# Modulation chunks in pairs of 1024 columns on VectorE, and layer 0's second-gate chunks moved to VectorE

## The chip, the cores and the metric

One core of one Trainium2 chip runs the whole program in one launch. The metric is the time of one execution on the device in microseconds (us); less is better. Time before: 3164.56 us, the median of 3 runs (3164.38 to 3165.99).

## The reference

Two layers of a diffusion backbone on a latent and a context stream of 256 tokens each, 2048 channels, everything in float32. Layer 0 mixes tokens by pooling in four groups of 512 channels (windows 2, 4, 8, 16); layer 1 is neighbourhood attention. Both are followed by a gated feed-forward block with 5504 inner channels. What the change touches is the modulation: in front of and behind every sub-layer stand a shift, a scale and a gate per channel, which come from one vector for each stream:

```
sc  = silu(c)            # latent stream, 2048 values;  silu(c_ctx) for the context stream
mod = sc @ w_mod[l] + b_mod[l]          # (2048) x (2048, 6 * 2048) for each layer l
shift1, scale1, gate1, shift2, scale2, gate2 = split(mod, 6)
h = h + gate1 * mixer(rms_norm(h, g1) * (1 + scale1) + shift1)
h = h + gate2 * conv_ffn(rms_norm(h, g2) * (1 + scale2) + shift2)
```

The matrix w_mod holds 2 x 2048 x 12288 float32 values, 201 MB, each of which is used once for each stream.

## The kernel before

**Layout.** Channels lie on the 128 partitions, so the 2048 channels are 16 tiles (KT). Matrix products run as three float32r products: every piece of weights (512 KB, 128 x 1024) is loaded by SP's queue into a room (`stage`), ScalarE makes its high part (L142, names ending in h) and VectorE the low part (L144, names ending in l); TensorE then does high x high, high x low, low x high. The rooms are 6 tiles of a staging pool (`wst`) and, in the first part of layer 0, tiles of the inputs A0 to A15 that aren't in use yet; `lend` says which. A room comes free when its last reader is done, and SP's queue is in order, so a transfer that waits for a room holds all later ones.

**Chunks.** The 12288 columns of a layer's modulation are 24 chunks of 512: chunks 0 to 3 are the first shift, 4 to 7 the first scale, 8 to 11 the first gate, 12 to 15, 16 to 19 and 20 to 23 the same for the second norm. A chunk's weights are 16 blocks of 128 x 512, 4 MB in 8 transfers. There are two ways to work one off:
- `mod_pe` (layer 0, all 24 chunks): 16 float32 matmuls with the 32-column tile `sc` as weights (L193), four side by side on quarters of the array, into one PSUM bank; then a copy by ScalarE (L198), four transposes on TensorE (L203), a reduction (L205) and the bias (L181) on VectorE.
- `mod_pieces` (layer 1): VectorE multiplies each 128 x 512 block by the stream's value per partition and adds it to `macc` (L219 for the first block, L221 for the rest). Chunks 0 to 7 are done for both streams (`two`, 32 instructions each), chunks 8 to 23 for the latent stream alone (`one`, 16 each). At a chunk's end VectorE transposes `macc` in blocks of 32 (L228) and reduces it (L229, tile `modr`); one small matmul with `quad` sums the quarters of the partitions (L165, tile `modt_<chunk>s`, issued ahead of other work by `tc.high_priority`), and VectorE adds the bias (L181).

**Order.** Both are generators, and each `next` on them issues one step (a quarter of a chunk). Layer 0's mixer and the first 8 feed-forward tiles run in four groups g = 0 to 3 (`partial`, 32 half tiles each): within group g TensorE contracts the 512 channels of that group (tiles `cg` and `cu`, weights `wcg`, `wcu`), while the mixer of group g + 1 and its chunks (`need`) are issued between the half tiles (`between`). The inputs `Ad` of group g + 1 come out of that mixer. In group 3 the chunks still open are the four of the second gate (20 to 23). The end of group 3 on VectorE is `late` (L328). After that come the other feed-forward tiles: for each four of them `gu0` (gate and up products, L601 to L603, PSUM banks `gu`), then `down0` in four parts mg (L625 to L627, weights `wd_0` to `wd_3`, banks `d`), and every such step takes one step of `mod_pieces` with it. The bank tag `d` has three banks and a fourth from tag `m`, taken in turn by the down tiles and the sums `modt`. Then the tile scheduler of the language orders the instructions of each engine; each engine runs its own in that order.

Of the kernel before, what the change touches and what calls it, by code (L numbers as in the profile page):

```python
# [10 lines left out]
F32 = mybir.dt.float32  # L11
F32R = mybir.dt.float32r
# [24 lines left out]
# half tiles of the last group at which the second norm and the first gates are done  # L37
# [3 lines left out]
# columns of the packed per-channel array: (name, columns)  # L41
# [16 lines left out]
def kernel(ctx: ExitStack, tc: tile.TileContext, xT, cxT, wmod, wg, wu, wd, wp,  # L58
# [35 lines left out]
    # silu(c), silu(c_ctx)  # L94
# [25 lines left out]
    def load(src, cols, name):  # L120
        """[128, cols] in pieces of up to 1024 columns"""
# [8 lines left out]
    def split(ts, name, share=0):  # L130
        """float32 pieces -> list of (hi, lo); share: one lo in so many on GpSimd"""
# [24 lines left out]
    def by_row(ps):  # L156
        """four transposed tiles whose columns 32 j + s hold four parts of stream s: [128, 4, s, j]"""
        return ps.rearrange("p (i j c) -> p i c j", i=4, j=4)[:, :, 0:2, :]

    def quarter_sum(x, n, name):  # L160
        """x: [32 j + c, (tile, b), n streams], parts j of the sum for the channel 32 b + c of the tile; for each
        quarter of the partitions a view [32 channels, tiles, streams]"""
        with tc.high_priority():
            ps = bank("d", f"{name}s")
            nc.tensor.matmul(ps[:, : 16 * n].rearrange("p (k s) -> p k s", s=n), quad, x, start=True, stop=True)  # L165
# [3 lines left out]
    def finish_mod(l, ch, streams, src):  # L169
        """bias added to the views of quarter_sum; scales turn into factors"""  # L170
# [16 lines left out]
    def mod_pe(l, ch, sc, pool):  # L187
        """512 columns of one modulation matrix, both streams, on TensorE"""
# [19 lines left out]
    def mod_pieces(todo, pool):  # L208
        """the same for the chunks of todo, on VectorE, one weight piece per step"""
        for l, ch, streams in todo:  # L210
            acc = {s: pool.tile([P, 512], F32, tag=f"macc{s}", bufs=1, name=f"macc{s}_{l}_{ch}") for s in streams}
            for g in range(4):
                ts = load(lambda a, b: wmod[l, ch, g, :, a:b], 2048, f"wm{l}_{ch}_{g}")
                for j in range(4):
                    k = 4 * g + j
                    w = ts[j // 2][0][:, 512 * (j % 2) : 512 * (j % 2) + 512]
                    for s in streams:
                        if k == 0:
                            nc.vector.tensor_scalar(acc[s], w, sc2[:, k, s : s + 1], None, op0=ALU.mult)  # L219
                        else:  # L220
                            nc.vector.scalar_tensor_tensor(acc[s], w, sc2[:, k, s : s + 1], acc[s],  # L221
                                                           op0=ALU.mult, op1=ALU.add)
                if g == 3:
                    n = len(streams)
                    r = pool.tile([P, 16, 2], F32, tag="modr", bufs=2, name=f"modr_{l}_{ch}")[:, :, 0:n]
                    for s in streams:
                        t = f0.tile([P, 512], F32, tag="t2", name=f"modu{s}_{l}_{ch}")
                        nc.vector.transpose(t, acc[s])  # L228
                        nc.vector.tensor_reduce(out=r[:, :, s], in_=t.rearrange("p (k r) -> p k r", r=32), axis=AX.X,  # L229
                                                op=ALU.add)  # L230
                yield
            finish_mod(l, ch, streams, quarter_sum(r, n, f"modt_{l}_{ch}"))
# [5 lines left out]
    class Norm:  # L238
        """sum of squares over channels, fed one channel tile at a time; then 1 / rms on all partitions"""
# [37 lines left out]
    def normalise(l, which, h_of, streams, rstd, pool, ks=range(KT), keep=A):  # L277
        """A[k] = float32r parts of rstd * h * (1 + scale) * g + shift, per stream"""
# [15 lines left out]
    # ================= layer 0 =================  # L294
# [879 lines left out]
```

## Time and profile before

| what | us |
|---|---|
| median of 3 runs | 3164.56 |
| span of the profiled execution | 3160.8 |
| what lies around the span, against the median | 3.8 |
| first loads and group 0's chunks and mixer | 0 to 80 |
| group 0 of layer 0 (first to last product on its inputs, about) | 80 to 167 |
| groups 1, 2, 3 (about) | 167 to 257, 257 to 348, 348 to 440 |
| other feed-forward tiles of layer 0 without modulation steps | 440 to 617 |
| the same with steps of `mod_pieces` | 617 to 1700 |
| layer 1: attention, feed-forward | 1740 to 2390, 2390 to 3160 |

The profile is of one execution, whose own time isn't given apart from its span. TensorE (PE) is busy for 97% of the span and its granted clock is 0.990 of full speed, so the span is read as TensorE's work plus the places where TensorE waits. VectorE (DVE) is busy for 64%. A row of a group says: line, engine, operation, output <- inputs, shape, count, then busy time and mean duration of one in ns, then the engine's idle time ahead of it and what ended it.

### The profile page before, as it was taken

How to read it: one execution, taken by the hardware profiler on the slowest of the kernel's cores; microseconds unless marked ns; L12 is line 12 of the kernel's file. 1: busy time of each engine (PE TensorE's matmuls, PEld its weight loads, DVE VectorE, ACT ScalarE, POOL GpSimd, SP SyncE). 2: the span in 40 equal slices, each digit the busy share in tenths (PEclk: the TensorE clock that was granted, in tenths of full speed). 3: DMA queues.
4: the chain of work that ended last, by engine and by line, in shares of the span. 5: the costliest groups of instructions: out<-in, count | busy, mean ns of one | idle time of the engine just before them, and what ended most of it. 6: DMA issues, size and time to landing. Idle time of an engine off the chain costs nothing.

```text
span 3160.8 us, 40908 instructions
## 1 busy us (share of the span) xinstructions
PE 3064.6 (97%) x15082; PEld 2410.6 (76%) x15082; DVE 2037.9 (64%) x2886; ACT 1353.6 (43%) x2187; POOL 940.3 (30%) x843
## 2 busy tenths in 40 slices
PE   6999999999999999999999999999999999999998
PEld 2565568887877778777787777777778888888887
DVE  4445664387686775868675665574777676666666
ACT  3333454323333232323324443343445665556665
POOL 2011213303123040413313000000002477667776
PEclk9999999999999999999999999999999999999999
DMA  9878663375564655556563333232345555555553
GB/s 376 330 270 315 207 206 100 111 229 183 170 199 159 202 171 189 187 167 199 164 202 114 102 105 106 96 109 94 104 141 179 176 193 184 196 185 182 180 182 119
DMA packets 161545, 559.72 MB, mean 177 GB/s; under 512 B 17600, under 2 KB 22208, under 8 KB 161344
## 3 DMA queue, kind: packets, MB, share of 16 engines
q1 hardware_dynamic: 161344, 557.10, 52.9%
q8 instruction: 119, 1.95, 0.2%
q14 instruction: 82, 0.67, 0.1%
HBM read 554.93 MB, written 2.10 MB: 176 GB/s over the span
## 4 chain that ended last, share of the span: by engine, by line
PE 69%; DVE 12%; DMA 12%; issue 4%; POOL 2%; ACT 1%; SPq 0%; DVEq 0%; POOLq 0%; ACTq 0%
DMA wm<-wmod 11%; DVE macc L221 6%; PE g L731 5%; PE u L731 4%; PE d L776 4%; PE mod L193 3%; PE d L627 3%; PE d L625 3%; PE d L626 3%; PE g L732 3%; PE u L732 2%; PE d L777 2%; PE k L895 2%; PE k L896 2%; PE q L915 2%
## 5 line engine op out<-in xcount | busy, mean ns | idle before, releaser
L221 DVE SCALAR_TENSOR_TENSOR macc<-wm,sc,macc 128x512 f32<-128x512 f32 x480 | 411.9, 883 | 225.7 <-DMA wm<-wmod 221.2
L638 POOL TENSOR_TENSOR hl<-hl,dy 128x256 f32<-128x256 f32 x160 | 164.8, 1030 | 931.5 <-ACT dy L637 930.6
L788 POOL TENSOR_TENSOR hl<-hl,dy 128x256 f32<-128x256 f32 x320 | 323.2, 1044 | 45.3 <-ACT dy L786 43.7
L637 ACT ACTIVATE dy<-d,modT 128x256 f32<-128x256 f32 x320 | 133.2, 470 | 172.7 <-PE d L627 162.1
L638 POOL TENSOR_TENSOR hc<-hc,dy 128x256 f32<-128x256 f32 x160 | 180.1, 1125 | 0.0
L193 PE MATMUL mod<-wm,sc 128*32 128x512 f32 x768 | 135.9, 613 | 24.6 <-DMA wm<-wmod 24.6
L344 ACT ACTIVATE sg<-g 128x512 f32<-128x512 f32 x43 | 27.2, 632 | 299.0 <-DVE g L341 299.0
L869 POOL TENSOR_TENSOR rk<-rk,rp 128x256 f32<-128x256 f32 x16 | 12.7, 795 | 372.8 <-DVE rk L868 314.4
L786 ACT ACTIVATE dy<-d,modT 128x512 f32<-128x512 f32 x160 | 103.5, 686 | 29.8 <-PE d L777 24.8
L439 POOL TENSOR_TENSOR pf<-ws,inv 128x256 f32<-128x256 f32 x32 | 28.4, 906 | 221.4 <-DVE ws L434 153.0
L144 DVE TENSOR_TENSOR wd_2l<-wd,wd_2h 128x1024 fp32r<-128x1024 f32 (+1 forms) x44 | 57.0, 1300 | 46.5 <-ACT wd_2h L142 45.7
L193 PEld LDWEIGHTS mod<-wm,sc 128*32 128x32 f32 x768 | 23.7, 109 | 80.8 <-issue 58.1
L755 DVE TENSOR_TENSOR actb<-sgb,actb 128x256 fp32r<-128x256 f32 x43 | 68.2, 1586 | 20.8 <-ACT actb L754 20.2
L627 PE MATMUL d<-act,wd_0l 128*128 128x512 f32 x172 | 69.7, 406 | 12.1 <-DVE wd_0l L144 12.1
L144 DVE TENSOR_TENSOR wd_0l<-wd,wd_0h 128x1024 fp32r<-128x1024 f32 (+1 forms) x44 | 53.9, 1227 | 37.8 <-ACT wd_0h L142 37.1
L142 ACT CAST wd_0h<-wd 128x1024 fp32r<-128x1024 f32 (+1 forms) x44 | 45.3, 1031 | 67.9 <-PE g L602 35.9
L626 PE MATMUL d<-act,wd_0h 128*128 128x512 f32 x172 | 69.1, 402 | 0.0
L625 PE MATMUL d<-act,wd_3h 128*128 128x512 f32 x172 | 68.0, 395 | 1.1 <-DVE modT L181 1.1
L625 PE MATMUL d<-act,wd_0h 128*128 128x512 f32 x172 | 69.0, 402 | 0.0
L625 PE MATMUL d<-act,wd_2h 128*128 128x512 f32 x172 | 67.9, 395 | 0.1
L626 PE MATMUL d<-act,wd_2h 128*128 128x512 f32 x172 | 68.0, 395 | 0.0
L627 PE MATMUL d<-act,wd_1l 128*128 128x512 f32 x172 | 68.0, 395 | 0.0
(1753 smaller groups left out, 10024.1 us busy)
## 6 DMA issues: line engine op xcount, KB each, us to landing
wm<-wmod SPq DMA_DIRECT2D x384, 512.0 KB, 5.2
wd<-wd SPq DMA_DIRECT2D x168, 512.0 KB, 4.5
wg<-wg SPq DMA_DIRECT2D x156, 512.0 KB, 4.0
wu<-wu SPq DMA_DIRECT2D x156, 512.0 KB, 4.7
wv<-wv SPq DMA_DIRECT2D x32, 512.0 KB, 3.6
wk<-wq SPq DMA_DIRECT2D x32, 512.0 KB, 3.8
wq<-wq SPq DMA_DIRECT2D x32, 512.0 KB, 3.7
wo<-wo SPq DMA_DIRECT2D x32, 512.0 KB, 3.7
```

The costliest lines, as they stand in the source:

```text
L144: eng.tensor_tensor(lo[:, :n], t[:, :n], hi[:, :n].bitcast(F32), op=ALU.subtract)
L193: nc.tensor.matmul(ps[32 * j : 32 * j + 32, :], sc[:, 4 * g + j, :], ts[j // 2][0][:, 512 * (j % 2) : 512 * (j % 2) + 512], start=(g == 0) ...
L221: nc.vector.scalar_tensor_tensor(acc[s], w, sc2[:, k, s : s + 1], acc[s], op0=ALU.mult, op1=ALU.add)
L625: nc.tensor.matmul(ps, hi[:, o : o + P], xh, start=(i == 0), stop=False)
L626: nc.tensor.matmul(ps, hi[:, o : o + P], xl, start=False, stop=False)
L627: nc.tensor.matmul(ps, lo[:, o : o + P], xh, start=False, stop=(i == n - 1))
L637: nc.scalar.activation(y[:, s], ps[:, T * s : T * s + T], AF.Copy, scale=M(0, 5, k, s))
L638: nc.gpsimd.tensor_tensor(h_of(s)[:, k, :], h_of(s)[:, k, :], y[:, s], op=ALU.add)
L731: nc.tensor.matmul(ps, hi[:, c : c + P], flat(B[k]), start=(k == 0), stop=False)
L732: nc.tensor.matmul(ps[:, T:], lo[:, c : c + P], B[k][:, 0], start=False, stop=(k == KT - 1))
L776: nc.tensor.matmul(ps, hi[:, o : o + P], flat(acts[i]), start=(i == 0), stop=False)
L788: nc.gpsimd.tensor_tensor(hl[:, k, :], hl[:, k, :], y[:, q], op=ALU.add)
```

## The change

Three things change.
1. `mod_pieces` becomes `mod_pairs`. The latent-only chunks 8 to 23 of layer 1 are done two at a time: a transfer brings one block of two neighbouring chunks (two rows of 2 KB for each partition instead of one of 4 KB), and one instruction works on 128 x 1024. The chunks for both streams stay at 128 x 512. A step still has two transfers of 512 KB; a pair has 8 steps. Both streams' sums, or a pair's, now share one tile `macc` of 128 x 1024, of which there is one.
2. The small matmul and the bias (`ending`) are issued one step later, behind the next step's VectorE work, and without `tc.high_priority`.
3. Layer 0's chunks 20 to 23 leave `mod_pe` and become two pairs for both streams on VectorE, in front of layer 1's chunks. Their sums lie in the input tiles A2, A3 and A6, A7, which are therefore no longer lent as rooms. Their 16 steps and the last ending are issued at every fourth half tile from group 1's third to group 3's third, where before their steps were issued in group 3.

```diff
-        with tc.high_priority():
-            ps = bank("d", f"{name}s")
-            nc.tensor.matmul(ps[:, : 16 * n]..., quad, x, start=True, stop=True)
+        ps = bank("d", f"{name}s")
+        nc.tensor.matmul(ps[:, : 16 * n]..., quad, x, start=True, stop=True)
...
+    def mod_pairs(todo):
+        ending = None
+        for l, ch, m, streams, accs in todo:
+            if not m:
+                ending()
+                ending = None
+                yield
+                continue
+            n = len(streams)
+            acc = accs(f"macc_{l}_{ch}", m)
+            for step in range(4 * m):
+                for piece in (2 * step, 2 * step + 1):
+                    w = stage(f"wm{l}_{ch}_{piece}")
+                    if m == 1:
...
+                    else:
+                        g, j = divmod(piece, 4)
+                        nc.sync.dma_start(w.rearrange("p (c n) -> p c n", c=2),
+                                          wmod[l, ch : ch + 2, g, :, 512 * j : 512 * j + 512].rearrange("c p n -> p c n"))
+                        ks = [(piece, w)]
+                    for k, v in ks:
+                        for s in streams:
+                            if k == 0:
+                                nc.vector.tensor_scalar(acc[s], v, sc2[:, k, s : s + 1], None, op0=ALU.mult)
+                            else:
+                                nc.vector.scalar_tensor_tensor(acc[s], v, sc2[:, k, s : s + 1], acc[s],
+                                                               op0=ALU.mult, op1=ALU.add)
+                if ending is not None:
+                    ending()
+                    ending = None
+                if step == 4 * m - 1:
...
+                    for c in range(m):
+                        for s in streams:
+                            t = f0.tile([P, 512], F32, tag="t2", name=f"modu{s}_{l}_{ch}_{c}")
+                            nc.vector.transpose(t, acc[s][:, 512 * c : 512 * c + 512])
+                            nc.vector.tensor_reduce(out=r[:, c, :, s], in_=t..., axis=AX.X, op=ALU.add)
+                    def ending(l=l, ch=ch, m=m, streams=streams, n=n, r=r):
+                        for c in range(m):
+                            finish_mod(l, ch + c, streams, quarter_sum(r[:, c, :, 0:n], n, f"modt_{l}_{ch + c}"))
+                yield
+        ending()
...
+        def in_inputs(a, b):
+            def accs(name, m):
+                return [ap0.tile([P, 1024], F32, tag=f"A{k}", name=f"{name}_{k}") for k in (a, b)]
+            return accs
+        def in_pool(name, m):
+            t = mp.tile([P, 1024], F32, tag="macc", bufs=1, name=name)
+            return [t, t] if m == 2 else [t[:, 0:512], t[:, 512:1024]]
+        two = [(1, q, 1, both, in_pool) for q in range(8)]
+        one = [(1, q, 2, (0,), in_pool) for q in range(8, 24, 2)]
+        pump = mod_pairs([(0, q, 2, both, in_inputs(a, a + 1)) for q, a in ((20, 2), (22, 6))]
+                         + [(0, 24, 0, (), None)]
+                         + [x for t in zip(two, one) for x in t])
...
-                for q in range(4):
-                    yield from mod_pe(0, 20 + q, sc, f0)
...
-                lend((range(8, KT), [*range(12, KT), *range(4)], range(8), ())[g])
+                lend((range(8, KT), [*range(12, KT), 0, 1], (0, 1, 4, 5), ())[g])
...
+                    if half % 4 == 2 and 32 < 32 * g + half < 100:
+                        next(pump, None)
...
-            need(97)
+            need(81)
```

How the order of the engines' instructions changes shows at three places. In these rows a number behind a name is a buffer's or a chunk's, and "x2" says that a row stands for two alike.

VectorE in the feed-forward tiles of layer 0, where the down product wd_3 begins (chunk 11 or pair 10 ends there, chunk 2 begins). Before:

```order
L221 SCALAR_TENSOR_TENSOR macc_1_11_6384<-wm_11_3_1024_6627,sc_81,macc_1_11_6384 128x512 x2
L144 TENSOR_TENSOR wd_3_0l_6526<-wd_3_0_0_6521,wd_3_0h_6525 128x1024
L219 TENSOR_SCALAR macc_1_2_6729<-wm_2_0_0_6730,sc_81 128x512
L144 TENSOR_TENSOR wd_3_0l_6530<-wd_3_0_1024_6523,wd_3_0h_6529 128x1024
L221 SCALAR_TENSOR_TENSOR macc_1_2_6729<-wm_2_0_0_6730,sc_81,macc_1_2_6729 128x512
L339 SCALAR_TENSOR_TENSOR g_19_6511<-g_19_6393,vt,g_19_6511 128x2x255
L341 SCALAR_TENSOR_TENSOR g_19_6511<-g_19_6393,vt,g_19_6511 128x2x255
L221 SCALAR_TENSOR_TENSOR macc_1_2_6729<-wm_2_0_1024_6732,sc_81,macc_1_2_6729 128x512 x2
```

After:

```order
L236 SCALAR_TENSOR_TENSOR macc_10_6060<-wm_10_15_6593,sc_81,macc_10_6060 128x1024
L144 TENSOR_TENSOR wd_3_0l_6493<-wd_3_0_0_6488,wd_3_0h_6492 128x1024
L144 TENSOR_TENSOR wd_3_0l_6497<-wd_3_0_1024_6490,wd_3_0h_6496 128x1024
L364 SCALAR_TENSOR_TENSOR g_19_6478<-g_19_6362,vt,g_19_6478 128x2x255
L366 SCALAR_TENSOR_TENSOR g_19_6478<-g_19_6362,vt,g_19_6478 128x2x255
L144 TENSOR_TENSOR wd_3_1l_6583<-wd_3_1_0_6578,wd_3_1h_6582 128x1024
```

The first block of chunk 2 stood between the two low parts of wd_3_0; now chunk 2 shares `macc` with the pair before it and begins only behind that pair's transposes, after wd_3_2's first low part.

TensorE, the sum of chunk 2. Before, in the middle of the gate product of tile 20:

```order
L602 MATMUL g_20_6934<-A_0_3_3567,wg_20h_6918 128x512
L603 MATMUL g_20_6934<-A_0_3_3567,wg_20l_6919 128x512
L165 MATMUL modt_2s<-modr_2_7007,quad 128x32
L601 MATMUL g_20_6934<-A_0_3_3585,wg_20h_6918 128x512
L602 MATMUL g_20_6934<-A_0_3_3585,wg_20h_6918 128x512
```

After, behind the up product of tile 20:

```order
L641 MATMUL u_20_6986<-A_0_3_3605,wu_20h_6963 128x512
L642 MATMUL u_20_6986<-A_0_3_3605,wu_20l_6964 128x512
L164 MATMUL modt_2s<-modr_2_6979,quad 128x32
L640 MATMUL g_21_7071<-A_0_3_3080,wg_21h_7049 128x512
L641 MATMUL g_21_7071<-A_0_3_3080,wg_21h_7049 128x512
```

The sum moved back by more than a whole product of 48 matmuls. Those of a pair (`modt_10s`, `modt_11s`) now stand one behind the other between the down parts wd_3_1 and wd_3_2, where before chunk 11's stood alone inside wd_3_1 and chunk 10's in an up product.

VectorE in group 1 of layer 0, from the additions of the first up tiles (`part<-part,cu`) to the low part of the second weights wcg_4. Before:

```order
L531 TENSOR_TENSOR part_612<-part_612,cu_0_1487 128x512
L144 TENSOR_TENSOR wcg_4l_1609<-wcg_4_0_1604,wcg_4h_1608 128x1024
L531 TENSOR_TENSOR part_637<-part_637,cu_1_1511 128x512
L144 TENSOR_TENSOR wcg_4l_1613<-wcg_4_1024_1606,wcg_4h_1612 128x1024
L205 TENSOR_REDUCE modT_2_1523<-modt_2_1518 128x8
```

After:

```order
L236 SCALAR_TENSOR_TENSOR macc_20_3_1360<-wm_20_5_1533,sc_81,macc_20_3_1360 128x1024
L236 SCALAR_TENSOR_TENSOR macc_20_2_1359<-wm_20_6_1598,sc_81,macc_20_2_1359 128x1024
L236 SCALAR_TENSOR_TENSOR macc_20_3_1360<-wm_20_6_1598,sc_81,macc_20_3_1360 128x1024
L236 SCALAR_TENSOR_TENSOR macc_20_2_1359<-wm_20_7_1602,sc_81,macc_20_2_1359 128x1024
L236 SCALAR_TENSOR_TENSOR macc_20_3_1360<-wm_20_7_1602,sc_81,macc_20_3_1360 128x1024
L144 TENSOR_TENSOR wcg_4l_1643<-wcg_4_0_1638,wcg_4h_1642 128x1024
```

Twelve instructions of 128 x 1024 on chunks 20 and 21 (blocks 2 to 7) now stand between the addition of cu_0 and the first low part of wcg_4. On SP's queue six of their transfers (blocks 2 to 7) and four others now stand ahead of wcg_4's two.

More of the change, by code (lines that the diff above doesn't have):

```diff
@@ L160, in quarter_sum @@
     def quarter_sum(x, n, name):
-        with tc.high_priority():
-            ps = bank("d", f"{name}s")
-            nc.tensor.matmul(ps[:, : 16 * n].rearrange("p (k s) -> p k s", s=n), quad, x, start=True, stop=True)
+        ps = bank("d", f"{name}s")
+        nc.tensor.matmul(ps[:, : 16 * n].rearrange("p (k s) -> p k s", s=n), quad, x, start=True, stop=True)
         v = ps[:, : 16 * n].rearrange("p (i b s) -> p i b s", b=4, s=n)
@@ L206, in mod_pe @@
         finish_mod(l, ch, both, [r])
[L208 to L230, printed above, removed]
-                yield
-            finish_mod(l, ch, streams, quarter_sum(r, n, f"modt_{l}_{ch}"))
@@ L346, in gate0 @@
             if f == NS - 1:
-                a = [mp.tile([P, 512], F32R, tag=f"macc{j}", bufs=1, name=f"act_{f}_{j}") for j in range(2)]
+                a = mp.tile([P, 2, 512], F32R, tag="macc", bufs=1, name=f"act_{f}")
             else:
                 a = act_tile(f"act_{f}", F32R)
-                a = [a[:, 0], a[:, 1]]
+            a = [a[:, 0], a[:, 1]]
             nc.scalar.copy(a[0], sg)
@@ L585 @@
         extra.append(whx)
-        two = [(1, q, both) for q in range(8)]
-        one = [(1, q, (0,)) for q in range(8, 24)]
-        pump = mod_pieces([x for t in zip(two, one[::2], one[1::2]) for x in t], mp)
         def gu0(f):
```

9 lines of the change are left out of this document (added).

## The prediction

> **What bounds the kernel now.** First the page, for the span, the engines' shares and what the transfers moved in each fortieth of the span:
>
> ```profile
> span 3160.8 us, 40908 instructions
> PE 3064.6 (97%) x15082; PEld 2410.6 (76%) x15082; DVE 2037.9 (64%) x2886; ACT 1353.6 (43%) x2187; POOL 940.3 (30%) x843
> GB/s 376 330 270 315 207 206 100 111 229 183 170 199 159 202 171 189 187 167 199 164 202 114 102 105 106 96 109 94 104 141 179 176 193 184 196 185 182 180 182 119
> ```
>
> TensorE has work for 97% of the span, so a change counts where it takes work from TensorE or ends a wait of TensorE. Next the busy time in stretches: groups 1, 2, 3 of layer 0, what follows them, and the long stretch in which VectorE works off layer 1's chunks beside the feed-forward tiles. The columns are the stretch, then busy time and count of PE, PEld, DVE, ACT, POOL, the granted clock, the transfers' share and GB/s.
>
> ```profile
> 167.00:257.00 90.00, 88.48 (x500) 54.41 (x499) 49.09 (x84) 30.31 (x55) 13.50 (x15) 1.00 0.80 278
> 257.00:348.00 91.00, 91.00 (x507) 54.48 (x505) 53.19 (x90) 32.31 (x58) 16.23 (x18) 1.00 0.71 255
> 348.00:440.00 92.00, 91.40 (x475) 48.23 (x474) 67.64 (x126) 46.70 (x90) 21.34 (x15) 1.00 0.80 269
> 440.00:507.00 67.00, 66.35 (x287) 54.04 (x288) 35.48 (x49) 38.59 (x73) 25.59 (x29) 1.00 0.31 102
> 700.00:1660.00 960.00, 930.38 (x4024) 755.96 (x4023) 694.66 (x874) 309.04 (x472) 252.68 (x224) 0.99 0.56 183
> ```
>
> In the groups TensorE never pauses to speak of, and VectorE has 103 of 273 us free (273 - 49.1 - 53.2 - 67.6). In the long stretch TensorE is idle for 960 - 930.4 = 29.6 us. The chain of waits of TensorE says on what, there (us in total, times, longest):
>
> ```profile
> PE d L627 <- DVE wd_0l L144: 12.1, 6, 3.0
> PE modt_1s L165 <- DVE modr L229: 3.9, 1, 3.9
> PE g L603 <- DVE wg_24l L144: 2.0, 1, 2.0
> PE modt_6s L165 <- DVE modr L229: 1.7, 1, 1.7
> PE modt_7s L165 <- DVE modr L229: 1.6, 1, 1.6
> PE g L603 <- DVE wg_32l L144: 1.4, 1, 1.4
> PE g L603 <- DVE wg_28l L144: 1.3, 1, 1.3
> PE g L603 <- DVE wg_20l L144: 1.2, 1, 1.2
> PE modt_4s L165 <- DVE modr L229: 1.1, 1, 1.1
> PE d L625 <- DVE modT L181: 1.1, 1, 1.1
> PE modt_5s L165 <- DVE modr L229: 1.1, 1, 1.1
> PE modt_2s L165 <- DVE modr L229: 1.1, 1, 1.1
> ```
>
> Three kinds: a sum that comes before its `modr` (six rows, 10.5 us), the low part of wd_0 (12.1 us), and the low part of the gate weights behind a burst of `macc` work (5.9 us). VectorE itself idles there on transfers:
>
> ```profile
> DVE macc L221 <- DMA wm<-wmod: 206.1, 80, 5.4
> DVE macc L219 <- DMA wm<-wmod: 43.8, 14, 4.7
> ```
>
> **Part 1: chunks 20 to 23 leave TensorE.** Groups 0 to 3 hold 20 chunks of the matmuls (632 records) and their transposes:
>
> ```profile
> L193 PE MATMUL mod<-wm,sc 128*32 128x512 f32 x632 | 104.4, 601 | 0.4 <-DMA wm<-wmod 0.4
> L203 PE MATMUL modt<-ident,modev 128*128 128x128 f32 x80 | 12.0, 273 | 1.4 <-ACT modev L198 1.4
> ```
>
> A chunk is 104.4/20 + 12.0/20 = 5.8 us, four are 23 us, all of it in group 3. Four small sums come in; their price lies between nothing and a chunk's transposes (0.6 each), and I take 0.3 each since one matmul replaces four. So TensorE has 22 us less: 251 instead of 273 us in groups 1 to 3.
>
> **Part 2: the same chunks come to VectorE**, 64 instructions of 128x1024 with their tails, in groups 1 and 2, on an engine that had 103 us free. The prices, by start-to-start times of VectorE and by the rows of tails:
>
> ```profile
> 973.14 0.75 DVE L221 SCALAR_TENSOR_TENSOR macc<-wm,sc,macc 128x512 f32<-128x512 f32 x1 [4.35 <-DMA wm<-wmod]
> 973.80 1.22 DVE L144 TENSOR_TENSOR wu_23l<-wu,wu_23h 128x1024 fp32r<-128x1024 f32 x1
> 974.94 0.74 DVE L221 SCALAR_TENSOR_TENSOR macc<-wm,sc,macc 128x512 f32<-128x512 f32 x1
> ...
> L229 DVE TENSOR_REDUCE modr<-modu 128x16 f32<-128x512 f32 x28 | 18.9, 676 | 0.2
> L228 DVE STREAM_TRANSPOSE modu<-macc 128x512 f32<-128x512 f32 x28 | 18.9, 693 | 0.1
> L144 DVE TENSOR_TENSOR wd_3l<-wd,wd_3h 128x1024 fp32r<-128x1024 f32 x14 | 21.8, 1560 | 0.0
> L144 DVE TENSOR_TENSOR wd_0l<-wd,wd_0h 128x1024 fp32r<-128x1024 f32 x15 | 18.3, 1218 | 0.0
> L181 DVE TENSOR_TENSOR modT<-modt_5s,vt x4: 154/162/171, 1328.1 to 1328.6; 32x8 f32<-32x8 f32 x4
> L205 DVE TENSOR_REDUCE modT<-modt 128x8 f32<-128x32 f32 x20 | 3.7, 187 | 34.6 <-PE modt L203 34.6
> ```
>
> No row shows the accumulation at 1024 columns. It lies between the subtraction of the same shape (973.80 to 974.94: 1.14) and two of 512 (973.14 to 973.80: 0.66 each, 1.32). I take 1.2, near the same shape. 60 x 1.2 = 72 us; four first multiplications at no more than that, 3 us; 8 transposes and 8 reductions 8 x (0.69 + 0.68) = 11 us; 16 bias adds at 0.16, 2.6 us; less four reductions of 0.19. That is 88 us. The rows wd_3l (1560 ns, while GpSimd adds) and wd_0l (1218 ns, while it rests) bound what GpSimd costs each: 0 to 0.34, so 0 to 20 us. GpSimd is busy for 51 of the 273 us, a fifth, so 4 us. VectorE then has 170 + 92 = 262 us of work in groups 1 to 3, where TensorE has 251: **VectorE becomes the bound.** And it can't be busy throughout:
>
> ```profile
> 167.00:217.00 50.00, 49.92 (x301) 28.96 (x303) 19.30 (x37) 13.21 (x25) 2.43 (x2) 1.00 0.74 254
> 357.00:367.00 10.00, 10.00 (x48) 4.90 (x47) 3.85 (x10) 1.17 (x2) 2.15 (x2) 1.00 0.68 226
> ```
>
> From 167 to 217 it has 19.3 us of work and gets four steps of 4 x 1.2 us: 11 us stay free. At 357 to 367 the second norm's own chain goes round by TensorE, GpSimd and ScalarE: 6 us free. 262 + 17 = 279 against 273 before, 6 us more. A microsecond of it can run over into 440 to 507, where VectorE has half its time free. I take **+5 us**. The lower end is TensorE's 251 (-22); the upper end comes with rival 2 (+40).
>
> What this hides behind: the low parts of wcg_4 in group 1, the additions to `part` that free PSUM banks, and `Ad` and `late` at each group's end all queue behind the new instructions, and TensorE waits for each of them. What comes free with shorter transfers in group 3 gains nothing while VectorE sets the pace.
>
> The transfers of the four chunks, 32 x 0.524 = 16.8 MB, go ahead to groups 1 and 2, which move 278 x 90 + 255 x 91 = 48.2 MB: 65.0 MB in 181 us are 359 GB/s. The page's fullest slice has 376, so they fit with 8 us to spare, over 10 to 12 rooms in place of 14. The two-row form of a transfer moves the same bytes; I cost it at nothing, and 359 against 376 is the cover.
>
> The Trainium skill, page "DMA: Bandwidth & Descriptors", section "Bandwidth", says that transfers from HBM are bound on the HBM side at about 358 GB/s a core. By that the 65.0 MB take 181.6 us and the sum stays where it is, with no spare at all; the 376 of the first slice disagrees and decides here, and the rule speaks for rival 2.
>
> **Part 3: sums a step later.** The six waits for `modr` go, since the sums now stand behind a whole up product or down part: **-10.5 us**.
>
> **Part 4: pairs and one `macc`.** This is where the wait for wd_0 comes from; VectorE above, TensorE below, when the down products of one four begin:
>
> ```profile
> 980.83 1.22 DVE L144 TENSOR_TENSOR wd_0l<-wd,wd_0h 128x1024 fp32r<-128x1024 f32 x1
> 986.46 0.49 DVE L219 TENSOR_SCALAR macc<-wm,sc 128x512 f32<-128x512 f32 x1 [4.41 <-DMA wm<-wmod]
> 986.86 1.22 DVE L144 TENSOR_TENSOR wd_0l<-wd,wd_0h 128x1024 fp32r<-128x1024 f32 x1
> ...
> 985.33 0.40 PE L626 MATMUL d<-act,wd_0h 128*128 128x512 f32 x1
> 988.14 0.50 PE L627 MATMUL d<-act,wd_0l 128*128 128x512 f32 x1 [2.41 <-DVE wd_0l L144]
> ```
>
> The next chunk's first multiplication waits 4.41 us for its block, with wd_0's second low part behind it. After the change nothing stands between the two: **-12.1 us**. Two things are late next. Chunk 2's 32 instructions begin only behind the pair's transposes, but before the gate weights of the next four there are 21 accumulations now and 23 before, so the 5.9 us of the gate stay. And a pair's two sums hold two of the four banks in turn until their bias adds, so the third tile of wd_2 can wait. The row of such a wait is `d L625 <- modT`, 1.1 us once; the ends are 0 and 3 us in each of 8 rounds. I take 0.75, nearer to that row: **+6 us**. The 128 instructions saved by pairs (128 x (1.32 - 1.2) = 15 us of VectorE and more beside GpSimd) lie where VectorE waits 250 us for transfers: nothing.
>
> **Sum.** 3160.8 + 5 - 10.5 - 12.1 + 6 = 3149.2; with the 3.8 us that the median has above the span, **3153 us** (-0.4%).
>
> **Rivals.** 1. VectorE keeps up, since work is reordered into its gaps: the front gains its 22 us, 3160.8 - 22 - 16.6 + 3.8 = 3126. For it: 103 us free, 92 needed. Against: the 17 us that can't be filled, and in-order queues. 2. Slower: an accumulation on chunks 20 to 23 waits for its transfer, as 94 of them did in the long stretch (249.9 us, 2.7 each), and the low part of wcg_4 waits behind it. One such wait in each of 16 steps is 43 us; with 5 us counted already and some inside waits that are there anyhow, about 25 us on top: 3178. It decides from 18 us on top (3171). For it: 359 of 376 GB/s, fewer rooms, six of the new transfers ahead of wcg_4's. Against: VectorE is late there, so blocks have time to land. 3. The long stretch keeps its 29.6 us, as banks or gate weights take over the waits: 3160.8 + 5 + 3.8 = 3170, or 3166 with a quarter of the 16.6 gained. For it: VectorE is full ahead of every gate wait. 4. The sums don't go later in effect because the bias adds hold banks instead; it is within 3.
>
> **How the numbers follow.** The forecast (3141 to 3163) has 0.45, rival 1 0.2, rival 2 0.15, rival 3 0.12, others 0.08. A measurement tells this kernel's change from none beyond about 0.2%, 6.3 us. Faster (under 3158): 0.8 of the forecast, rival 1 and half of the others, 0.60. Slower (over 3171): rival 2 and a little, 0.17. Same: 0.23. The range 3129 to 3174 leaves out the best of rival 1 and the worst of rival 2.
>
> **What would show it.** Right: VectorE over 85% busy from 167 to its `late`, TensorE with waits of 15 to 35 us in groups 1 to 3 on wcg_4l, `Ad`, `part` or `late`, the first gate product of tile 8 at 440 to 450; no rows `modt <- modr`, none of wd_0l behind L234. Wrong: that gate product at 425 or before (rival 1), waits on `wm` by VectorE ahead of 440 over 20 us (rival 2), waits `d <- modT` or `g <- wgl` over 15 us in the long stretch (rival 3).

## The result, and the profile after

| | us |
|---|---|
| before, median of 4 runs | 3164.97 |
| after, median of 4 runs (3264.58 to 3277.72) | 3272.88 |
| ratio, 95% interval | 1.0334 (1.0317 to 1.035) |
| forecast | 3153 (3129 to 3174) |

The change makes the kernel 108 us slower. The page of the changed kernel, to be held against the first block of the prediction:

```profile
span 3262.8 us, 40633 instructions
PE 3077.7 (94%) x14946; PEld 2420.4 (74%) x14946; DVE 2083.3 (64%) x2846; ACT 1345.5 (41%) x2183; POOL 918.2 (28%) x843
```

VectorE's share is the same 64%, TensorE's falls from 97 to 94%: it is idle for 185 us of the span in place of 96. Its busy time rises too, by 13 us, though four chunks' work has left it; its mean granted clock is 0.982 in place of 0.990. So this isn't more work, it is waiting, with slower products behind some of the waits. The busy times of the changed kernel in groups 1, 2 and 3 (cut at the first gate product of each) and in the long stretch, with the columns as before:

```profile
175.30:283.00 107.70, 96.02 (x484) 55.97 (x484) 86.93 (x117) 30.65 (x55) 16.47 (x16) 0.97 0.88 306
283.00:394.20 111.20, 101.08 (x501) 56.25 (x500) 90.08 (x133) 30.02 (x53) 15.55 (x16) 0.94 0.81 279
394.20:469.90 75.70, 60.46 (x309) 44.23 (x307) 68.66 (x127) 41.57 (x80) 19.63 (x14) 0.94 0.36 116
700.00:1740.00 1040.00, 970.57 (x4124) 778.64 (x4123) 679.24 (x771) 309.12 (x477) 226.19 (x224) 0.98 0.57 173
```

Cut in the same way, the groups of the kernel before last 91.0, 89.4 and 88.3 us; its rows, cut to the microsecond:

```profile
172.00:263.00 91.00, 89.56 (x501) 54.81 (x501) 50.34 (x86) 32.05 (x57) 14.90 (x16) 1.00 0.80 277
263.00:352.00 89.00, 89.00 (x495) 53.65 (x492) 51.41 (x88) 30.27 (x55) 14.44 (x16) 1.00 0.70 252
352.00:441.00 89.00, 87.75 (x451) 47.33 (x449) 64.74 (x121) 44.01 (x84) 19.30 (x13) 1.00 0.82 280
```

Groups 1 and 2 grow by 17 and 22 us and group 3 shrinks by 13. Tile 8 starts at 469.9 us in place of 440.6: 29 us late. In the three groups TensorE's idle time is 37.0 us (2.7 before), and it is busy for 257.6 us (266.3 before). With the 22 us of work gone that the prediction estimates, 244 would do; some 13 us more go to the granted clock, which is 0.97, 0.94 and 0.94 here and was 1.00. From 239 us on it stands at 0.50 in five stretches of 6.8 us, the last of which runs past tile 8's start.

The two profiled spans differ by 102 us (the medians by 108). The rest, some 73 of the 102, is lost behind the start of tile 8, where TensorE runs 12902 products in both kernels: 53 us are more idle time, 20 are longer busy time for the same products. In the long stretch TensorE is now idle for 1040 - 970.6 = 69.4 us (29.6 before). Its chain of waits there:

```profile
PE u L642 <- DVE wu_27l L144: 3.6, 2, 2.5
PE u L642 <- DVE wu_39l L144: 3.4, 2, 2.7
...
PE u L642 <- DVE wu_18l L144: 1.9, 1, 1.9
PE g L642 <- DVE wg_34l L144: 1.7, 1, 1.7
...
PE d L666 <- DVE wd_0l L144: 0.2, 1, 0.2
```

The waits for `modr` are gone, and those for wd_0 are down to 0.2 us there; one more of 6.1 us stands behind 1740. In their place 19 up tiles wait for their low part (55 us in all) and ten gate tiles (13 us). VectorE, which should have made those low parts, sits idle for 317 us in the same stretch, more than the 250 before:

```profile
DVE macc L236 <- DMA wm<-wmod: 317.4, 94, 6.3
```

The chain of work in 28 us of a pair's steps says how (start us, us, what; "issue" is time in which nothing is waited for that the profile shows):

```profile
956.26 1.23 DVE wu_21l L144
957.50 0.02 issue
957.51 6.14 DMA wm<-wmod
...
963.74 1.30 DVE macc L236
965.04 0.02 issue
965.05 4.94 DMA wm<-wmod
...
971.22 1.23 DVE wg_22l L144
972.45 0.02 issue
972.46 4.80 DMA wm<-wmod
...
977.36 1.29 DVE macc L236
978.65 0.02 issue
978.67 5.57 DMA wm<-wmod
```

Each piece of `wmod` starts 0.02 us after a VectorE instruction has given up a room, and VectorE does nothing on the chain until that piece has landed. One piece is under way at a time; a step has two, so it pays two landings one after the other, while the transfers' share is 0.57 (173 GB/s). In VectorE's order a low part of the weights stands between the two accumulations, and TensorE waits for that low part.

A wait of TensorE costs more than its own length at times, as these rows of TensorE show (start us, us):

```profile
963.79 0.39 PE L640 MATMUL u<-A,wu_21h 128*128 128x512 f32 x1
964.02 0.40 PE L641 MATMUL u<-A,wu_21h 128*128 128x512 f32 x1
967.53 0.80 PE L642 MATMUL u<-A,wu_21l 128*128 128x512 f32 x1 [3.12 <-DVE wu_21l L144]
968.13 0.63 PE L640 MATMUL u<-A,wu_21h 128*128 128x512 f32 x1
968.55 0.63 PE L641 MATMUL u<-A,wu_21h 128*128 128x512 f32 x1
968.98 0.63 PE L642 MATMUL u<-A,wu_21l 128*128 128x512 f32 x1
```

Products start every 0.23 us before the wait and every 0.43 after it: the granted clock is 0.50 from 966.3 to 973.1 us. From 760 to 1720 us there are 9 such stretches at 0.50, of 3.4 or 6.8 us, each at a wait of TensorE, and they add some 13 us; before there were 4, some 6 us. Not every wait has one: 18 waits are longer than 2 us, and 8 of them are among the 9. The Trainium skill, page "TensorE: Matmul & The Clock Gate", section "What's actually happening", says that an idle window of some 3.4 us, which runs free, halves the clock. The halving agrees; but of the 9 waits 8 were only 1.9 to 2.6 us long, shorter than such a window, and there the measurement decides.

### The profile page after: what moved, and what is told of

Same layout as the page of the kernel before. It is cut to its first block, busy times and chain, and to the rows that moved or that the text cites. A ratio compares the mean times of both kernels' runs of the same rounds, so it can differ in the third digit from the quotient of the medians.

```text
span 3262.8 us, 40633 instructions
## 1 busy us (share of the span) xinstructions
PE 3077.7 (94%) x14946; PEld 2420.4 (74%) x14946; DVE 2083.3 (64%) x2846; ACT 1345.5 (41%) x2183; POOL 918.2 (28%) x843
## 4 chain that ended last, share of the span: by engine, by line
PE 55%; DVE 17%; DMA 15%; issue 6%; POOL 2%; ACT 1%; DVEq 0%; SPq 0%; POOLq 0%; ACTq 0%
DMA wm<-wmod 13%; DVE macc L236 7%; PE g L770 5%; PE u L770 4%; PE d L815 4%; PE g L771 2%; PE d L664 2%; PE d L666 2%; PE d L665 2%; PE u L771 2%; PE d L816 2%; PE k L934 2%; PE k L935 2%; PE q L954 2%; PE k L936 2%
## 5 line engine op out<-in xcount | busy, mean ns | idle before, releaser
L236 DVE SCALAR_TENSOR_TENSOR macc<-wm,sc,macc 128x512 f32<-128x512 f32 (+1 forms) x420 | 450.6, 1114 | 347.3 <-DMA wm<-wmod 346.6
L677 POOL TENSOR_TENSOR hl<-hl,dy 128x256 f32<-128x256 f32 x160 | 148.6, 928 | 1025.8 <-ACT dy L676 1025.6
L827 POOL TENSOR_TENSOR hl<-hl,dy 128x256 f32<-128x256 f32 x320 | 327.0, 1053 | 44.4 <-ACT dy L825 42.8
L677 POOL TENSOR_TENSOR hc<-hc,dy 128x256 f32<-128x256 f32 x160 | 167.9, 1050 | 0.0
L192 PE MATMUL mod<-wm,sc 128*32 128x512 f32 x640 | 117.9, 635 | 32.2 <-DMA wm<-wmod 30.8
L908 POOL TENSOR_TENSOR rk<-rk,rp 128x256 f32<-128x256 f32 x16 | 12.7, 795 | 374.1 <-DVE rk L907 315.6
L376 ACT CAST act<-sg 128x512 fp32r<-128x512 f32 x43 | 26.6, 619 | 219.2 <-DVE sg L370 219.1
L794 DVE TENSOR_TENSOR actb<-sgb,actb 128x256 fp32r<-128x256 f32 x43 | 60.5, 1406 | 20.2 <-ACT actb L793 19.9
L664 PE MATMUL d<-act,wd_1h 128*128 128x512 f32 x172 | 68.6, 399 | 2.8 <-ACT dy L676 2.8
L664 PE MATMUL d<-act,wd_2h 128*128 128x512 f32 x172 | 68.3, 397 | 0.0
L665 PE MATMUL d<-act,wd_1h 128*128 128x512 f32 x172 | 68.1, 396 | 0.0
```

What stands on the lines that cost most here:

```text
L192: nc.tensor.matmul(ps[32 * j : 32 * j + 32, :], sc[:, 4 * g + j, :], ts[j // 2][0][:, 512 * (j % 2) : 512 * (j % 2) + 512], start=(g == 0) ...
L236: nc.vector.scalar_tensor_tensor(acc[s], v, sc2[:, k, s : s + 1], acc[s], op0=ALU.mult, op1=ALU.add)
L664: nc.tensor.matmul(ps, hi[:, o : o + P], xh, start=(i == 0), stop=False)
L665: nc.tensor.matmul(ps, hi[:, o : o + P], xl, start=False, stop=False)
L677: nc.gpsimd.tensor_tensor(h_of(s)[:, k, :], h_of(s)[:, k, :], y[:, s], op=ALU.add)
L827: nc.gpsimd.tensor_tensor(hl[:, k, :], hl[:, k, :], y[:, q], op=ALU.add)
```

## The experiments

Times are medians, with the ratio to the runs of the kernel before on the same chip (its median there: 3162.5 to 3166.3) and its 95% interval.

**The two parts apart.** First the layer-1 part alone (`mod_pe` gets chunks 20 to 23 back, with their `need` and `lend`):

```diff
+                for q in range(4):
+                    yield from mod_pe(0, 20 + q, sc, f0)
...
-        pump = mod_pairs([(0, q, 2, both, in_inputs(a, a + 1)) for q, a in ((20, 2), (22, 6))]
-                         + [(0, 24, 0, (), None)]
-                         + [x for t in zip(two, one) for x in t])
+        pump = mod_pairs([x for t in zip(two, one) for x in t])
```

> Only the layer-1 part of the change: chunks 20 to 23 of layer 0 are back on TensorE with their old rooms, the pairs, the one accumulator tile and the sums a step later stay. The trace of the changed kernel has the start of tile 8 late by 29 us, the long stretch (tiles 16 to 42) longer by 57 and its end by 13 more. Theory A (the layer-1 part by itself makes the long stretch longer): 3164 + 57 to 70 = 3221 to 3234 us, and VectorE waits for wm in 700 to 1740 us for some 300 us as in the changed kernel. Rival B (the long stretch is slower only because it starts late or with other rooms, after the moved chunks): within 10 us of the kernel before.

Measured: 3237.7 us, 1.023 (1.0215 to 1.0246), +74 us, a little above theory A's range. Then the layer-0 part alone, with `mod_pieces` for layer 1:

```diff
-                         + [x for t in zip(two, one) for x in t])
+        two = [(1, q, both) for q in range(8)]
+        one = [(1, q, (0,)) for q in range(8, 24)]
+        pump = mod_pieces([x for t in zip(two, one[::2], one[1::2]) for x in t], mp)
```

> Only the layer-0 part: chunks 20 to 23 on VectorE in pairs, layer 1 by 512-column chunks with the old sums. Theory A (the two parts add up): tile 8 starts late by 29 us, the long stretch is as before, 3164 + 25 to 35 = 3189 to 3199 us. Rival B: the time is mostly in layer 1 after the moved chunks, this kernel comes out over 3215 us.

Measured: 3197.1 us, 1.0106 (1.0091 to 1.0121), +33 us. The parts add up to 107 of 108 us, so each is studied by itself.

**The long stretch: the order.** The accumulations of a step are put behind the low parts:

```diff
-                eng.tensor_tensor(lo[:, :n], t[:, :n], hi[:, :n].bitcast(F32), op=ALU.subtract)
+                lows[:] = [eng.tensor_tensor(lo[:, :n], t[:, :n], hi[:, :n].bitcast(F32), op=ALU.subtract).ins]
...
+                    with ExitStack() as behind:
+                        for ins in lows if l == 1 else ():
+                            behind.enter_context(tc.issue_after(ins))
```

VectorE's order at tile 35, without and with it:

```
L236 SCALAR_TENSOR_TENSOR macc_18 <- wm_18_13          L145 TENSOR_TENSOR        wu_35l <- wu_35_0
L144 TENSOR_TENSOR        wu_35l <- wu_35_0            L374 TENSOR_TENSOR        sg
L236 SCALAR_TENSOR_TENSOR macc_18 <- wm_18_14          L145 TENSOR_TENSOR        wu_35l <- wu_35_1024
L370 TENSOR_TENSOR        sg                           L240 SCALAR_TENSOR_TENSOR macc_18 <- wm_18_10
L144 TENSOR_TENSOR        wu_35l <- wu_35_1024         L381 TENSOR_TENSOR        act
L377 TENSOR_TENSOR        act                          L240 SCALAR_TENSOR_TENSOR macc_18 <- wm_18_11
```

> The layer-1 part as in the run above, with one thing added: an accumulation of a step is put behind both low parts of the weights that the step loads, where the changed kernel has low part, accumulation, low part, accumulation. Theory A (the alternation lets one piece of wmod at a time be under way, since each piece's room is the one that the low part just ahead has left, so a step pays two transfers of 5 us one after the other): the waits of u and g in the long stretch fall from 63 to under 35 us and the time comes to 3150 to 3180 us. Rival B (the two-row transfer of 2 KB rows is what is late): no lower than 3210 us. Rival C (the 1024-wide instruction by itself, which needs both rows): no lower than 3210 us.

Measured: 3121.6 us, 0.9863 (0.9846 to 0.9879): 116 us less than the same part without the order, and 42 less than the kernel before, further down than theory A's range. TensorE has no wait left in the long stretch:

```profile
700.00:1660.00 960.00, 960.00 (x4203) 786.20 (x4202) 683.34 (x783) 333.89 (x513) 265.58 (x255) 1.00 0.62 190
```

Two-row transfers and 1024-wide instructions are all in it, so neither is bad by itself, and rivals B and C are out as causes on their own. The same edit in `mod_pieces` of the kernel before, and nothing else:

> The kernel before with nothing but the order changed: the 512-column accumulations of a step behind both low parts of the weights that the step loads; the sums stay where they were. Theory A (it is the place of the accumulations among the low parts that lets TensorE idle in the long stretch, and the sums a step later matter little): most of the 29.6 us of idle and of the slow clock behind it go, 3120 to 3137 us. Rival D (the run above was fast because of the sums a step later, the pairs or the one accumulator tile): 3145 to 3165 us.

Measured: 3121.3 us, 0.987 (0.9854 to 0.9886), with this one wait left in the long stretch:

```profile
PE modt_1s L166 <- DVE modr L233: 1.7, 1, 1.7
```

So the chain was in the kernel before too and made its 29.6 us of idle time. With the order mended, pairs, the one `macc` and the later sums are worth nothing (3121.6 against 3121.3). This version beats both kernels.

**The long stretch: the transfers.** The layer-1 part with pieces of one row, the order of every engine's instructions unchanged:

```diff
-                        nc.sync.dma_start(w.rearrange("p (c n) -> p c n", c=2),
-                                          wmod[l, ch : ch + 2, g, :, 512 * j : 512 * j + 512].rearrange("c p n -> p c n"))
+                        nc.sync.dma_start(w, wmod[l, ch + j % 2, g, :, 1024 * (j // 2) : 1024 * (j // 2) + 1024])
```

> The layer-1 part with the same 1024-wide accumulations and the same order, but each piece of a pair is 1024 neighbouring columns of one chunk (4 KB rows, as before the change) and not 512 columns of two chunks; the modulation values of the pairs are other ones by it. Rival B (two-row transfers are late): back to within 12 us of the kernel before. Theory A (alternation): within 12 us of the layer-1 part, 3215 to 3240 us.

Measured: 3169.5 us, 1.0016 (1.0006 to 1.0026), +6 us. Rival B is right here: 68 of the 74 us come with the two-row form. Theory A as put falls: the same alternation with one-row pieces is hardly worse than the kernel before. It takes both, an order in which landings are paid one after the other, and pieces that land late. What makes a piece late was then split; here a piece has two rows of 2 KB from one chunk:

```diff
-                                          wmod[l, ch : ch + 2, g, :, 512 * j : 512 * j + 512].rearrange("c p n -> p c n"))
+                                          wmod[l, ch + j % 2, g].rearrange("p (c h n) -> h p c n", c=2, h=2)[j // 2])
```

> The layer-1 part, where each piece of a pair is again two rows of 2 KB for each partition, but both from one chunk, 4 KB apart instead of 4 MB; the modulation values of the pairs are other ones by it. If the shorter rows make the piece late: landing 4.6 us at least and 3225 to 3245 us as in the layer-1 part. If the distance between the rows does: landing from 3.5 us as in the one-row form and 3160 to 3180 us.

Measured: 3196.1 us, 1.0098 (1.0075 to 1.0122), +33 us, between both. The pieces in the three runs (issue, and from there to landing), layer-1 part, one row, near rows:

```profile
L228 SPq DMA_DIRECT2D wm<-wmod x100: 378/379/650, 762.1 to 1659.2; - x100
DMA to landing us min/median/max: 4.6/5.3/7.2
```

```profile
L229 SPq DMA_DIRECT2D wm<-wmod x109: 327/328/328, 760.7 to 1655.3; - x109
DMA to landing us min/median/max: 3.5/4.7/6.2
```

```profile
L228 SPq DMA_DIRECT2D wm<-wmod x106: 539/550/626, 759.6 to 1658.1; - x106
DMA to landing us min/median/max: 3.9/4.8/6.4
```

Of the pieces that had no other transfer under way when they were issued (about 30 in each run), the median is 5.19, 3.63 and 4.08 us. The pieces of chunks 0 to 7, which are one row in every run, landed in 3.70 us in the layer-1 part itself (22 of them). So shorter rows cost 0.4 us a piece, the 4 MB between the rows 1.1 more. Landing is counted from the start of the issue, and the issue of near rows is itself 0.22 us longer (550 against 328 ns), so a part of the 0.4 may be the issue's. Lateness of 0, 0.4 and 1.6 us goes with +6, +33 and +74 us. The Trainium skill, page "DMA: Bandwidth & Descriptors", section "Latency and other measured facts", says that copies between HBM tensors slow down when the rows of the partitions lie a large power of two apart, 4 MiB among them, and recover with a few KiB of padding. The direction agrees; the case differs, as here it is the two rows of one partition, and why isn't shown.

**The sums.** The kernel before with its sums a step later:

```diff
-        with tc.high_priority():
-            ps = bank("d", f"{name}s")
+        ps = bank("d", f"{name}s")
...
-            finish_mod(l, ch, streams, quarter_sum(r, n, f"modt_{l}_{ch}"))
+                    def ending(l=l, ch=ch, streams=streams, n=n, r=r):
+                        finish_mod(l, ch, streams, quarter_sum(r, n, f"modt_{l}_{ch}"))
```

> The kernel before, with one thing changed: each chunk's sum on TensorE comes a step later and without priority, as in the changed kernel. By the prediction's term the six waits of the sums go, 10.5 us: 3150 to 3156 us. By the run with low parts first, which had no waits left with the sums where they were, those waits belong to the same chain of transfers, and something else would wait in their place: 3160 to 3167 us.

Measured: 3169.8 us, 1.0017 (1.0007 to 1.0028): the 10.5 us of the prediction's term are not gained. The waits for `modr` are gone, and these stand in their place:

```profile
PE d L633 <- DVE wd_0l L144: 20.4, 6, 4.4
PE d L631 <- DVE modT L180: 3.0, 1, 3.0
```

The 12.1 us on wd_0 have become 20.4. Here a small wait of this chain that was taken away came back at the next place where TensorE needs VectorE.

**Groups 1 to 3.** The whole change with low parts first in both layers, then the change with only chunks 22 and 23 moved (one step at every eighth half tile, sums in A2 and A3) and low parts first in layer 1 alone:

```diff
-                        for ins in lows if l == 1 else ():
+                        for ins in lows:
...
-                         [(0, q, 2, both, in_inputs(a, a + 1)) for q, a in ((20, 2), (22, 6))]
+                         [(0, q, 2, both, in_inputs(a, a + 1)) for q, a in ((22, 2),)]
```

> The whole change with the low parts of the weights ahead of the accumulations in both layers. If the two parts add up, 3122 us of the layer-1 part with low parts first and the 33 us of the layer-0 part give 3150 to 3160 us, still a little faster than the kernel before. Rival (the order costs in groups 1 to 3 what it costs in the long stretch, so that the layer-0 part is good once it is mended): 3100 to 3120 us.

> As the run above, but only chunks 22 and 23 of layer 0 move to VectorE, over groups 1 and 2; chunks 20 and 21 stay on TensorE. Theory F (in groups 1 to 3 it is VectorE's own work that makes TensorE wait: 78 us of accumulations beside 174 us of other work in 281 us): half of it fits beside the rest, TensorE loses 11 us of work, and the time is 3108 to 3125 us. Rival G (any accumulation among the in-order work there costs a wait, whatever the total): 3130 to 3145 us.

Measured: 3157.3 us, 0.9982 (0.9973 to 0.9991), and 3144.7 us, 0.9944 (0.9929 to 0.9959). Against 3121.6 the moved chunks cost 36 us, and half of them 23. Rival G's range held, theory F's didn't. In the groups the edit of the first run doesn't help, but it leaves the order there nearly as it was: it puts an accumulation behind the low parts issued ahead of it, and in group 1 VectorE still runs 11 accumulations between the low parts of wcu_0 and the first of wcg_4 (12 without the edit). An order that puts wcg_4's low parts ahead of them was not tried.

Four runs of the layer-0 part alone then leave parts of its VectorE work and transfers out. With half of the accumulations, and with none of them but all transfers:

```diff
                         for s in streams:
+                            if l == 0 and s and k:      # second run: if l == 0 and k:
+                                continue
```

> The layer-0 part alone, with the same transfers, rooms and steps, but for the context stream only the first product of each chunk pair is formed: 30 accumulations of 128x1024 fewer (some 40 us of VectorE). Theory F (VectorE's work): the 33 us that the layer-0 part costs fall to 0 to 12, 3160 to 3176 us. Rival H (the transfers, the rooms that the pieces hold, or their place in SyncE's queue): 3188 to 3200 us as with all accumulations.

> The layer-0 part alone, with all transfers of its pairs, but only the first product of each pair and stream is formed: no accumulation of 128x1024 is left in groups 1 to 3 (78 us of VectorE fewer than in the layer-0 part). The layer-0 part cost 33 us, with half its accumulations 13. Theory F (VectorE's time, about half a microsecond lost for each added): 33 - 39 = -6, so 3150 to 3162 us, TensorE's 22 us of relief less what else is lost. Rival H (another part of the moved chunks keeps TensorE waiting: transfers, sums, transposes): 3165 to 3180 us.

Measured: 3177.2 us, 1.0049 (1.003 to 1.0068), and 3175.1 us, 1.0028 (1.0013 to 1.0044). The first half of the accumulations takes some 20 of the 33 us away, the second half some 4: theory F has the sign (the first run lies just above its range), not the proportion, and without any accumulation rival H's range held. Without the transfers too, and with the accumulations alone:

```diff
                 for piece in (2 * step, 2 * step + 1):
+                    if l == 0 and piece:
+                        for s in streams:               # second run only
+                            a_ = acc[s][:, 0:NVEC]
+                            nc.vector.scalar_tensor_tensor(a_, vt, sc2[:, piece, s : s + 1], a_, op0=ALU.mult, op1=ALU.add)
+                        continue
                     w = stage(f"wm{l}_{ch}_{piece}")
```

> The layer-0 part alone, of whose pairs only the first piece of each is loaded and multiplied: the other 30 transfers of 512 KB and the 60 accumulations are left out, the sums stay. Theory J (the transfers of the moved chunks, which fill the queues in groups 1 and 2, keep TensorE's own chunk products waiting there): the 22 us of TensorE's relief show, 3140 to 3150 us. Theory K (order, rooms or sums cost it): 3160 to 3178 us, as with the transfers.

> The layer-0 part alone, with all accumulations but without the 30 transfers: after the first piece of a pair each accumulation reads a tile of 936 columns that stays in SBUF, so 60 accumulations of 128x936 remain and no piece waits for a room or a landing. If VectorE's work and the transfers add up, the 33 us less the 31 of the transfers: 3155 to 3172 us. If VectorE's work alone makes the delay once it is all there: 3185 to 3200 us.

Measured: 3160.8 us, 0.9982 (0.9971 to 0.9993), and 3188.2 us, 1.0069 (1.0054 to 1.0084). Against the kernel before:

| layer-0 part | without transfers | with transfers |
|---|---|---|
| without accumulations | -3 us | +9 us |
| with accumulations | +24 us | +33 us |

Each cell is uncertain by 3 to 5 us. Accumulations cost 24 to 27 us, so VectorE's work makes most of the delay without any transfer, and the transfers make 9 to 12. The cell at -3 is the surprise: TensorE has 22 us less to do there, and theory J's gain didn't come. Group 3 of that run:

```profile
357.80:433.50 75.70, 61.81 (x304) 44.98 (x303) 67.46 (x125) 39.89 (x75) 19.47 (x13) 0.92 0.33 104
```

All the relief falls into this group, which shrinks by 12.6 us and not by 22. VectorE's own 67 us there (64.7 before) now fill 89% of it, which reads as the bound, though no run tries it. Groups 0 to 2 last 5 us longer than before, for which no run has the cause, and tile 8 starts 7 us early. With the transfers and no accumulations, groups 1 and 2 run the transfers at a share of 0.9:

```profile
171.00:270.20 99.20, 95.37 (x493) 55.07 (x493) 49.62 (x86) 31.44 (x57) 13.78 (x16) 0.98 0.91 318
270.20:381.00 110.80, 101.32 (x516) 56.10 (x512) 61.54 (x118) 32.69 (x61) 12.71 (x16) 0.97 0.89 308
```

There they last 99 and 111 us. The last two candidates in the groups are the form of the transfers and the rooms. The layer-0 part with one-row pieces (the transfer's edit above, in layer 0), and the kernel before with only the rooms of the changed one:

```diff
-                lend((range(8, KT), [*range(12, KT), *range(4)], range(8), ())[g])
+                lend((range(8, KT), [*range(12, KT), 0, 1], (0, 1, 4, 5), ())[g])
```

> The layer-0 part alone, each piece of its pairs being 1024 neighbouring columns of one chunk (4 KB rows), order and instructions otherwise the same; the modulation values of chunks 20 to 23 are other ones by it. In the long stretch a two-row piece with no other transfer under way took 5.2 us, a one-row piece 3.6. If the two-row form also makes groups 1 to 3 late, 3164 + 5 to 20; if VectorE's work does (theory F), no change against the layer-0 part: 3190 to 3203 us.

> The kernel before, with one thing changed: the rooms lent to transfers in groups 1 and 2 are those of the changed kernel (six and four tiles of inputs where there were eight each), with all chunks on TensorE as before. Rival H (a part of the 33 us is the rooms that the accumulators take away): 3170 to 3185 us. Theory F (VectorE's work and its order): within 6 us of the kernel before.

Measured: 3192.7 us, 1.0094 (1.0075 to 1.0113), and 3166.4 us, 1.001 (0.9999 to 1.002). The 4 us and the 2 us are inside the uncertainty, so neither is shown to be a cause.

## Why the prediction was wrong

The result lies 120 us above the forecast. By the runs 68 of them are the two-row transfers, some 22 are the sums and the one `macc` (-16.6 forecast with the banks, +6 measured with one-row pieces), and 28 are groups 1 to 3 (+5 forecast, +33 measured).

- **Two-row transfers "at nothing".** This is the step that failed. Its cover, 359 against 376 GB/s, speaks of bandwidth in the groups. In the long stretch what counted was the landing of a single piece: 5.2 us in place of 3.6, two in a row in each step. In the layer-1 part it is 68 of 74 us, and only with this order of VectorE's instructions: with low parts first the two-row form costs nothing (3121.6 against 3121.3).
- **Sums a step later, -10.5, and one `macc`, -12.1.** Both kinds of wait went from the long stretch, as said. But they weren't separate causes: all were places where the same chain of room, transfer and VectorE came late, and its delay moved to the next place (20.4 us on wd_0 when only the sums were moved, 55 us on the up tiles in the changed kernel). The wait row names the instruction at which a delay shows. VectorE's 250 us of waiting on `wm`, which the prediction quoted and read as spare time, was the chain itself.
- **Rival 3** kept the 29.6 us at most and asked for gate or bank waits (12.7 us on gate tiles, none on `modT`); that the idle time could more than double had no case.
- **Groups 1 to 3, +5.** The sizes were near: 246 us of VectorE work in the three windows above against 262, and for an accumulation there some 1.26 us from its start to the next instruction's against 1.2 (its row says 1.34, but neighbours overlap). What failed is the pooling of three groups into one balance, 262 + 17 against 273. TensorE's 22 us are all taken out of group 3, where VectorE's own 67 us seem to leave room for 13. The work is added in groups 1 and 2, where VectorE's 87 and 90 us meet TensorE's 90, and two engines that wait for each other in order (VectorE 27.6 us on TensorE's cg and cu in the three windows) filled 81% of VectorE's time there, not the 94% assumed. The transfers, costed at nothing, took 9 to 12 us. That products behind a wait run at half the clock had no term either; it is some 13 us in the three groups.
- **Banks, +6**, have no row in the long stretch.
- **The markers**: VectorE over 85% (it was 81, 81 and 91), waits of 15 to 35 us in groups 1 to 3 (11.7 + 10.1 + 15.2 = 37), tile 8 at 440 to 450 (469.9). These are TensorE's largest waits of the changed kernel from 160 to 470 us; `late` was foreseen, and wcu_4 stands where wcg_4l was expected:

```profile
PE cu L558 <- ACT wcu_4h L142: 8.3, 2, 4.9
PE mod L192 <- DMA wm<-wmod: 6.9, 5, 2.6
PE g L640 <- DVE late L353: 5.9, 1, 5.9
PE n2b L297 <- DVE n2d L295: 2.9, 1, 2.9
PE cu L560 <- DVE wcu_4l L144: 2.1, 2, 1.7
```

Rival 2's marker, over 20 us of VectorE waiting on `wm` ahead of 440, didn't come (7.5 us): an accumulation that waits for its landing with a low part behind it was the right mechanism in the wrong stretch.

## What to carry to other kernels

When an engine in the middle waits on transfers while bandwidth is free, follow one transfer from its issue to its landing to whoever waits behind it: if each is issued only when the last one's room is given up, the landings are paid one after the other, and a wait that is removed further down can come back at the next place, as it did here. Put the instructions that another engine waits for ahead of the filler in the in-order queue first; in the long stretch here both forms of the filler then ran 42 us faster than the kernel before. And balance engines stage by stage: here relief in group 3 didn't pay for load in groups 1 and 2.

## What the hardware showed that was not expected

A 512 KB piece that two rows of 2 KB for each partition make up, 4 MB apart, landed 1.6 us later than one with rows of 4 KB (5.2 against 3.6 us, nothing else under way), and 1.1 us of that go with the distance between the rows. Waits of TensorE of 1.9 to 2.6 us were enough for 3.4 us or more at a granted clock of 0.50, though only 8 of the 18 waits of over 2 us had such a stretch.
